# Low parts of the feed-forward weights by an accumulating DMA instead of a VectorE subtraction

## The chip, the cores and the metric

The kernel runs on one core of one Trainium2 chip. The metric is the device time of one execution in microseconds, the median of several runs. The core has five engines that run their own instruction streams and wait for each other by semaphores: PE (TensorE, matrix products; its weight loads are listed as PEld), DVE (VectorE), ACT (ScalarE), POOL (GpSimd) and SP (SyncE, which only issues DMAs here). Sixteen DMA engines move data between HBM and the on-chip memory SBUF. Products are summed in PSUM banks.

## The reference

Two transformer-like blocks on one sequence of 512 tokens with 1024 features, in float32. The first block has two layers: a convolution module in the first, attention with forget gates in the second, and after each of them the same feed forward and a gated projection:

```
hn = rmsnorm(h, ffn_norm[i])
h = h + jnp.square(jax.nn.relu(hn @ ffn_w1[i])) @ ffn_w2[i]      # 1024 -> 4096 -> 1024
```

The second block has three branches (a gated linear recurrence, block attention, attention to a memory), merges them and ends with a gated feed forward:

```
g = causal_dwconv(h @ w_ffn_gate, ffn_conv_w, ffn_conv_b)         # 1024 -> 3072
x = x + (jax.nn.gelu(g) * (h @ w_ffn_up)) @ w_ffn_down
```

The weights come in as float32.

## The kernel before, in words

**Products.** Activations lie feature-major: a tile is 128 features by 512 tokens. A float32 product is done with float32r operands, a shorter format: weight and activation are each split into a high part (rounded to float32r) and a low part (what rounding left), and `mm3` (line 356) issues three matmuls: high times high, high times low activation, low weight times high activation. `gemm` does this for the 8 k tiles of one output tile, so an output tile takes 24 matmuls.

**Panels.** All weights come in panels of 128 partitions by 2048 columns (1 MB), listed in the order of their use by `_panel_keys`. A panel of the feed forward holds 8 k tiles of 256 columns, so two output tiles, 48 matmuls. The feed-forward kinds are `w1` and `w2` (32 each over the two layers; for each of four chunks, four panels of `w1` and then four of `w2`), `gu` (24, a gate tile and an up tile each) and `dn` (12).

**How a panel gets ready.** `load` has SP fetch the raw panel into one of two raw buffers. `splitting` cuts it into four pieces of 512 columns; for each piece `part` has ScalarE copy the raw piece to `hi` (which rounds it) and VectorE, or for some kinds GpSimd, write `raw - hi` to `lo`. `hi` and `lo` have two buffers each. `panel(key)` makes sure that the split of this panel has been issued, and then calls `prefetch(i + 1, PREFETCH)`, which issues the load of the panel after the next and starts the split of the next one 3.0 us later.

**What sets the order.** Every engine executes its instructions in the order in which the program issues them. A planner, the class `Flow`, weaves them: it keeps an estimate of each engine's time, and side work (splits, norms, evacuations) is a generator that yields what its next step waits for. `flow.quiet(act, low, patience=HOLD)` lets a step go when the engines named are about free by the estimate, or after 1.2 us. These estimates only decide the order; what an instruction waits for on the chip are its real inputs.

**Around the panels.** `pairs` goes through the panels of a stage; in a stage's first panel the k tiles are the outer loop (`couter`), so that the panel can begin before all its input tiles are there. In the feed forward (line 826), VectorE takes the output tile out of PSUM (`z`), ScalarE squares it and rounds it, VectorE makes its low part. Norms run beside: ScalarE squares the stream's tiles (`sq`), GpSimd adds the squares up, VectorE makes the last addition, and PE forms the mean (`tp<-C,sq`). At the start of the second layer's feed forward the first `w1` panel's split is started by a `prefetch` with delay 0, behind the first half of the output projection's last tiles. The last two `dn` panels go token half by token half (256 columns): both panels for the first half, then both for the second; here `panel` of the last but one starts the split of the last.

Of the kernel before, what the change touches and what calls it, by code (L numbers as in the profile page):

```python
# [9 lines left out]
F32R = mybir.dt.float32r  # L10
BF = mybir.dt.bfloat16
AF = mybir.ActivationFunctionType
ALU = mybir.AluOpType
AX = mybir.AxisListType

S = 512
# [8 lines left out]

# [1 line left out]
_VECS = [  # L27
# [45 lines left out]
class Engine:  # L73
    """an engine whose instructions are issued in the order of the trace, with an estimate of when each one ends"""

# [48 lines left out]
class Flow:  # L124
    """Weaves side work into the stream of matrix products. Every engine issues in the order of this trace; a side is
    a generator that yields what its next step waits for: a time (us), tiles, or a condition."""

# [99 lines left out]
def kernel(ctx: ExitStack, tc, gain0, x_t, p_t, mem_t, vec, w, w_f, w_lru, rows, consts, out):  # L227
# [53 lines left out]

# [1 line left out]
    V = cp.tile([128, NV], F32, name="V")  # L283
# [11 lines left out]

# [1 line left out]
    raws, parts = {}, {}  # L297
# [9 lines left out]
    def part(i, k, pieces, low):  # L307
        """piece k of a panel's split, its low part on engine low"""
        if k == 0:
            parts[i] = tuple(wp.tile([128, PW], F32R, name=nm(n), tag=n, bufs=2) for n in ("hi", "lo"))  # L310
        r, (hi, lo), c = raws[i], parts[i], PW // pieces
        s = slice(c * k, c * k + c)
        gain = GAINED.get(_KEYS[i][0])
        if gain is not None:
            g = col(gain, k)
            act.activation(hi[:, s], r[:, s], AF.Copy, scale=g)
            dve.scalar_tensor_tensor(lo[:, s], r[:, s], g, hi[:, s].bitcast(F32), op0=ALU.mult, op1=ALU.subtract)
        else:
            act.copy(hi[:, s], r[:, s])
            low.tensor_sub(lo[:, s], r[:, s], hi[:, s].bitcast(F32))  # L320

    def splitting(i):
        pieces = KT if _KEYS[i][0] in GAINED else 4
        low = pool if _KEYS[i][0] in LO_POOL else dve
        c = PW // pieces
        for k in range(pieces):
            yield raws[i][:, c * k:c * k + c]
            yield flow.quiet(act, low, patience=HOLD)
            part(i, k, pieces, low)
# [17 lines left out]
    def panel(key, fetch=True):  # L347
        i = _PIDX[key]
        if i not in ahead:
            ahead[i] = flow.spawn(splitting(i), 0.0, 2)  # L350
        flow.finish(ahead[i])
        if fetch:
            prefetch(i + 1, PREFETCH)
        return parts[i]
# [6 lines left out]
    def gemm(ps, pan, c0, xs, width=256, ks=None, m=128):  # L361
        """ps += panel columns (from c0 of each k tile)^T x; ks: the k tiles of this call"""
        hi, lo = pan
        n = len(xs)
        for k in range(n) if ks is None else ks:
            if xs[k] is None:
                flow.until(lambda: xs[k] is not None)
            a = k * width + c0
            mm3(ps, hi[:, a:a + m], lo[:, a:a + m], xs[k][0], xs[k][1], k == 0, k == n - 1)

    def couter(pan, xs, ks=None, banks=None):
        """both output tiles of a panel, k tile by k tile"""
        banks = banks or [bank(), bank()]
        for k in range(len(xs)) if ks is None else ks:
            for j in range(2):
                gemm(banks[j], pan, 128 * j, xs, ks=[k])
        return banks

    def pairs(keys, xs):
        """output tiles of the panels in turn; the first panel k tile by k tile, while x still comes"""  # L380
        for i, key in enumerate(keys):
# [9 lines left out]

# [1 line left out]
    def split(src, g=None, n=S, scale=None):  # L393
        """exact two-part float32r split of src * g (g per feature)"""
        xh, xl = slot(F32R, "xh"), slot(F32R, "xl")
# [8 lines left out]
    def split_into(dst, k, src, g=None):  # L404
        """the same in steps, into dst[k]"""
        n = src.shape[-1]
# [12 lines left out]
    class Norm:  # L419
        """per-token mean over features of squares"""  # L420

# [48 lines left out]
    class Front:  # L470
        """input of a stage: gained splits of the stream's tiles as they come, and the norm's factor"""

# [36 lines left out]

# [1 line left out]
    G0 = cp.tile([128, KT], F32, name="G0")  # L511
# [32 lines left out]
    def diagonals(fs):  # L544
        """diagonal matrices of the last PE_TAPS[f] taps of a tile, both parts"""
        for f in fs:
# [27 lines left out]
    def conv_dve(order):  # L574
        """two tiles at a time, tap by tap in turn, so that none waits for its own sum; sums in PSUM"""
        todo, active = list(order), []
# [112 lines left out]

    # products that wait for nothing of the stream: ple projections, memory keys and values  # L690
    prd = dp.tile([KT, 128, S], F32, name="prd")

    def gemm32(ps, raw, c0, xs, width, m=128):
        """float32 products as they are, for panels whose splitting would hold other engines up"""
        n = len(xs)
        for k in range(n):
            a = k * width + c0
            pe.matmul(ps, raw[:, a:a + m], xs[k], start=k == 0, stop=k == n - 1)
# [61 lines left out]

    # layer norm over features, two passes
    ys = [None] * KT
# [56 lines left out]

# [1 line left out]
    def squared(z, k, t):  # L821
# [37 lines left out]

# [1 line left out]
    def diag(t, i):  # L861
        """query block i of transposed probabilities: key block j, query block i lies at column 384 j + 128 i"""
        a = t[:, 128 * i:128 * i + 128]
        return bass.AP(tensor=a.tensor, offset=a.offset, ap=[a.ap[0], [384, i + 1], [1, 128]])

    class Head:
        """causal attention of the head in rows 64 half.. of kt() and qt(); out() [128, S] takes a pair of heads"""

# [137 lines left out]
        def weigh(self):  # L1006
            """out[64 rows] = values^T probabilities^T; [V_hi | V_lo] or [V_lo | V_hi]"""
            vs = self.vs()
# [22 lines left out]
    class MemHead(Head):  # L1031
        """attention of one head of 128 features to the memory"""

# [48 lines left out]
    def attend(heads, period, gap):  # L1082
        """scores head by head, at least a period apart; all that follows as its inputs come"""
        state = {"scored": 0}
# [17 lines left out]
    def values(key, xs, r4):  # L1102
        """token-major values of 4 heads, split: per key block [128, 512]"""
        pan = panel(key)
        vs = []
        for b in range(4):
            ps = bank()
            token_major(ps, pan, xs, b)
            t = slot(F32R, "v")
            # heads 0,2: [hi|lo]; heads 1,3: [lo|hi]  # L1110
            v5 = t.rearrange("p (a b c d) -> p a b c d", a=2, b=2, c=2)
# [8 lines left out]

# [1 line left out]
    # the stream's tiles go in as they are, the gains into the weights; h is the sum of the two parts again  # L1122
    xs = front.xs
# [141 lines left out]

# [1 line left out]
    gg = small(8, "gg")  # L1267
# [47 lines left out]

    # gated linear recurrence
    xa, ga = [None] * 4, [None] * 4
# [10 lines left out]
    def recurrence():  # L1328
        # -8 softplus(-lam)
        lam = V[:, _VOFF["lam"]:_VOFF["lam"] + 4]  # L1330
# [53 lines left out]
        for f in range(4):  # L1384
# [4 lines left out]
            yield q  # L1389
            # 1 - a^2 = -tanh(log a) (1 + a^2)  # L1390
            dve.scalar_tensor_tensor(th[f], q, 1.0, th[f], op0=ALU.add, op1=ALU.mult)
# [24 lines left out]

    # block attention: of two blocks of 256 keys the past one is always chosen, so every earlier key counts
    rw, rr_ = slot(p="rows"), slot(F32R, "rowsr")
# [65 lines left out]

    # memory cross attention
    qx = [None] * 4
# [22 lines left out]

    # gated feed forward with a causal convolution on the gate  # L1510
    norms = [Norm(HALF) for _ in range(2)]
# [35 lines left out]

    # the last two panels token half by token half: the first one's norm and output go beside the second's products
    pre = [slot(p="out") for _ in range(2)]
# [64 lines left out]
MEM_PERIOD = 9.0  # L1614
LO_POOL = ("pw1", "vm", "o")


# [1 line left out]
def _pack(inp):  # L1619
# [3 lines left out]
    def wide(m, c0, n):  # L1623
        """columns c0..c0+n of m [K, N] as [128, K/128 * n]"""
        k = m.shape[0] // 128
# [96 lines left out]

    # shapes alone: identity, causal mask, 1/1024, distance rows
    consts = np.zeros((128, 257), np.float32)
# [41 lines left out]
```

## Time and profile before

| | |
|---|---|
| median of 3 runs | 2154.78 us (2154.36 to 2157.05) |
| profiled execution, span from first to last instruction | 2154.4 us |
| PE busy | 2109.2 us, 98% |
| VectorE busy | 1270.6 us, 59% |
| ScalarE busy | 937.4 us, 44% |
| GpSimd busy | 370.5 us, 17% |
| bytes moved by DMA | 204.79 MB, mean 95 GB/s |
| mean granted TensorE clock | 0.993 |

The profiled execution's own time is its span, 2154.4 us; the fastest run took 2154.36. Busy time is the time in which an engine executes; matmuls are pipelined, so one lasts longer in the list (390 ns) than the distance to the next, and the distance is what counts. In the rows a group is `out<-in` by the names in the program with the buffer numbers left out: `lo<-raw,hi` is the subtraction, `hi<-raw` the cast, `mm<-xh,lo` a matmul of a weight's low part. All instructions have line 83, since one helper issues them. In brackets stands the idle time of the engine before an instruction and what ended it. The stretch view gives, for each stretch, the busy time of each engine in it, the granted clock of TensorE as a share of 2.4 GHz, the DMA engines' mean share and their rate.

### The profile page before, as it was taken

To read this page: it belongs to the slowest core of one execution; us is meant where nothing else is said; L and a number is where in the kernel's file an instruction comes from. 1 tells how busy PE (TensorE), PEld (TensorE's weight loads), DVE (VectorE), ACT (ScalarE), POOL (GpSimd) and SP (SyncE) were. 2 spreads that over 40 slices of the span, in tenths; PEclk is the share of its full clock that TensorE was granted. 3 is DMA by queue.
4 is the path that set the end of the run, shared out by engine and by line. 5 is a ranking of instruction groups with operands and counts; after the bars stand their busy time and mean duration, and the time that the engine had idled before them with its cause. 6 is when DMAs were issued, how large, how long until landed. Compare 5 with 4: busy or idle time off the path is not lost. (4 is left out here: it accounts for less than half of the span.)

```text
span 2154.4 us, 26102 instructions
## 1 busy us (share of the span) xinstructions
PE 2109.2 (98%) x9920; PEld 1741.6 (81%) x9920; DVE 1270.6 (59%) x2166; ACT 937.4 (44%) x1884; POOL 370.5 (17%) x380
## 2 busy tenths in 40 slices
PE   7999999999999999999999999999999999999998
PEld 6867888888878887788888887778888888888887
DVE  5997534344576887544343567775564556465563
ACT  5766423233446676433232453665452333232222
POOL 5881100000121336300000031331010010000002
PEclk9999999999999999999999999999999999999999
DMA  5215232232222111222222233112222422222221
GB/s 183 98 45 190 86 110 80 97 104 92 98 80 85 61 61 60 79 98 98 98 93 89 95 125 129 71 64 95 98 79 79 142 93 98 100 96 98 95 101 59
DMA packets 38444, 204.79 MB, mean 95 GB/s; under 512 B 4648, under 2 KB 7976, under 8 KB 15920
## 3 DMA queue, kind: packets, MB, share of 16 engines
q1 hardware_dynamic: 37744, 202.62, 26.8%
q8 instruction: 78, 1.28, 0.2%
q10 hardware_dynamic: 576, 0.52, 0.1%
q14 instruction: 46, 0.38, 0.1%
HBM read 195.45 MB, written 7.68 MB: 94 GB/s over the span
## 5 line engine op out<-in xcount | busy, mean ns | idle before, releaser
L83 PE MATMUL mm<-xh,hi 128*128 128x512 f32 (+1 forms) x2544 | 991.5, 390 | 9.3 <-ACT hi L83 8.4
L83 PE MATMUL mm<-xl,hi 128*128 128x512 f32 (+1 forms) x2544 | 990.5, 389 | 0.0
L83 PE MATMUL mm<-xh,lo 128*128 128x512 f32 (+1 forms) x2544 | 990.0, 389 | 0.2
L83 PEld LDWEIGHTS mm<-xh,hi 128*128 128x128 f32 x2544 | 480.2, 189 | 105.0 <-ACT hi L83 8.4
L83 PEld LDWEIGHTS mm<-xh,lo 128*128 128x128 f32 x2544 | 480.1, 189 | 96.5 <-DVE lo L83 1.5
L83 PEld LDWEIGHTS mm<-xl,hi 128*128 128x128 f32 x2544 | 480.2, 189 | 94.3
L83 ACT CAST hi<-raw 128x512 fp32r<-128x512 f32 x636 | 354.3, 616 | 288.6 <-PE mm L83 268.9
L83 DVE TENSOR_TENSOR lo<-raw,hi 128x512 fp32r<-128x512 f32 x584 | 387.9, 713 | 50.3 <-ACT hi L83 48.8
L83 POOL TENSOR_TENSOR sq<-sq,sq 128x512 f32<-128x512 f32 (+1 forms) x69 | 84.7, 1230 | 1330.0 <-ACT sq L83 1329.4
L83 DVE TENSOR_TENSOR h<-mm,h 128x512 f32<-128x512 f32 (+1 forms) x113 | 75.6, 671 | 279.7 <-PE mm L83 279.6
L83 ACT ACTIVATE z<-z 128x512 f32<-128x512 f32 x64 | 40.4, 631 | 205.3 <-DVE z L83 205.3
L83 DVE SCALAR_TENSOR_TENSOR z<-mm,rbc 128x512 f32<-128x512 f32 x64 | 44.0, 690 | 120.7 <-PE mm L83 120.7
L83 POOL TENSOR_SCALAR P<-P,s 128x128 f32<-128x128 f32 (+2 forms) x112 | 65.3, 588 | 243.6 <-DVE s L83 151.0
L83 DVE TENSOR_TENSOR t<-mm,rbc 128x512 f32<-128x512 f32 x80 | 54.9, 688 | 82.5 <-PE mm L83 78.7
L83 DVE TENSOR_TENSOR xl<-z,xh 128x512 fp32r<-128x512 f32 x64 | 44.3, 693 | 74.7 <-ACT xh L83 74.7
L83 ACT ACTIVATE t<-t 128x512 f32<-128x512 f32 x40 | 25.2, 631 | 128.5 <-DVE t L83 128.4
L83 POOL TENSOR_TENSOR acc<-acc,tap 128x482 f32<-128x482 f32 (+29 forms) x60 | 77.3, 1288 | 13.1 <-ACT tap L83 9.5
L83 DVE SCALAR_TENSOR_TENSOR sc<-u,V,sc 128x511 f32<-128x511 f32 (+21 forms) x116 | 78.9, 732 | 0.5
L83 ACT ACTIVATE xh<-h,V 128x512 fp32r<-128x512 f32 x40 | 28.6, 722 | 112.4 <-DVE h L83 112.4
L83 POOL TENSOR_TENSOR lo<-raw,hi 128x512 fp32r<-128x512 f32 x52 | 69.6, 1363 | 38.8 <-ACT hi L83 38.6
L83 ACT CAST pth<-ptp 128x128 fp32r<-128x128 f32 (+2 forms) x112 | 46.1, 418 | 53.2 <-PE ptp L83 52.6
L83 ACT ACTIVATE P<-sc,s 128x128 f32<-128x128 f32 (+2 forms) x112 | 58.5, 524 | 18.1 <-DVE s L83 17.4
(228 smaller groups left out, 2235.8 us busy)
## 6 DMA issues: line engine op xcount, KB each, us to landing
raw<-in_w SPq DMA_DIRECT2D x175, 1024.0 KB
h<-in_x_t SPq DMA_DIRECT2D x8, 256.0 KB
prd<-pr SPq DMA_DIRECT2D x8, 256.0 KB
pr<-prd SPq DMA_DIRECT2D x8, 256.0 KB
resid<-h SPq DMA_DIRECT2D x8, 256.0 KB
h<-resid SPq DMA_DIRECT2D x8, 256.0 KB
out<-out SPq DMA_DIRECT2D x12, 128.0 KB
raw<-in_w SPq DMA_DIRECT2D x4, 256.0 KB
```

Source lines behind the costliest of these rows:

```text
L83: f(out, *args, **kw)
```

## The change

For the kinds `w1`, `w2`, `gu` and `dn`, the split goes another way. ScalarE writes `-raw` to the float32r tile `lo`, which rounds it, so that the tile holds minus the high part; after each two of the four pieces GpSimd issues a DMA that adds the raw weights, read from HBM a second time, to these 1024 columns. Then ScalarE makes the four casts to `hi`. VectorE has no part in it. `lo` gets three buffers for all kinds. A split of these kinds starts 0.2 us after its `prefetch`, not 3.0 us. The planner gets an estimate for the accumulating DMA. Comments and docstrings are taken out as well (not shown).

```diff
     def part(i, k, pieces, low):
         if k == 0:
-            parts[i] = tuple(wp.tile([128, PW], F32R, name=nm(n), tag=n, bufs=2) for n in ("hi", "lo"))
+            parts[i] = tuple(
+                wp.tile([128, PW], F32R, name=nm(n), tag=n, bufs=b) for n, b in (("hi", 2), ("lo", 3)))
...
+    def accumulate(out, src):
+        nc.gpsimd.dma_start(out, src, accum_op=ALU.add)
+        n = 4 * (out.size() if callable(out.size) else out.size)
+        flow.dma_t = max(flow.dma_t, flow.now, flow.when([out])) + n / 175e3
+        for k in flow.spans(out):
+            flow.ready[k] = flow.dma_t + 2.5
+
+    def splitting_dma(i):
+        r = raws[i]
+        parts[i] = hi, lo = tuple(
+            wp.tile([128, PW], F32R, name=nm(n), tag=n, bufs=b) for n, b in (("hi", 2), ("lo", 3)))
+        c = PW // 4
+        cut = [slice(c * k, c * k + c) for k in range(4)]
+        for k in range(4):
+            yield r[:, cut[k]]
+            yield flow.quiet(act, patience=HOLD)
+            act.mul(lo[:, cut[k]], r[:, cut[k]], -1.0)
+            if k % 2:
+                two = slice(c * k - c, c * k + c)
+                yield lo[:, two]
+                accumulate(lo[:, two], w[i, :, two])
+        for k in range(4):
+            yield flow.quiet(act, patience=HOLD)
+            act.copy(hi[:, cut[k]], r[:, cut[k]])
+
     def splitting(i):
+        if _KEYS[i][0] in LO_DMA:
+            yield from splitting_dma(i)
+            return
...
         if fetch:
-            prefetch(i + 1, PREFETCH)
+            prefetch(i + 1, 0.2 if _KEYS[min(i + 1, len(_KEYS) - 1)][0] in LO_DMA else PREFETCH)
...
+LO_DMA = ("w1", "w2", "gu", "dn")
```

## Rows read from the trace of the kernel before

**Rows 1.** Page, part 1: engine, busy us, share of the span, instructions.
```profile
PE 2109.2 (98%) x9920; PEld 1741.6 (81%) x9920; DVE 1270.6 (59%) x2166; ACT 937.4 (44%) x1884; POOL 370.5 (17%) x380
```

**Rows 2.** Stretches: length, busy PE PEld DVE ACT POOL (count), clock, DMA share, GB/s.
```profile
300.00:360.00 60.00, 60.00 (x266) 49.73 (x265) 23.16 (x37) 16.90 (x30) 0.00 (x0) 1.00 0.28 99
```

**Rows 3.** The same view, one panel of the first feed forward.
```profile
348.00:358.88 10.88, 10.88 (x49) 9.01 (x49) 5.18 (x8) 4.59 (x8) 0.00 (x0) 1.00 0.26 98
```

**Rows 4.** Page, part 5: costliest groups, busy us, mean ns, idle before, releaser.
```profile
L83 PEld LDWEIGHTS mm<-xh,lo 128*128 128x128 f32 x2544 | 480.1, 189 | 96.5 <-DVE lo L83 1.5
L83 ACT CAST hi<-raw 128x512 fp32r<-128x512 f32 x636 | 354.3, 616 | 288.6 <-PE mm L83 268.9
L83 DVE TENSOR_TENSOR lo<-raw,hi 128x512 fp32r<-128x512 f32 x584 | 387.9, 713 | 50.3 <-ACT hi L83 48.8
L83 ACT ACTIVATE xh<-h,V 128x512 fp32r<-128x512 f32 x40 | 28.6, 722 | 112.4 <-DVE h L83 112.4
```

**Rows 5.** Stretch view, entry of the second layer's feed forward.
```profile
906.04:913.90 7.86, 7.86 (x27) 6.89 (x28) 1.91 (x4) 0.24 (x2) 1.39 (x1) 0.50 0.41 146
```

**Rows 6.** Timeline there: start us, us, engine, operation, count [idle before <-releaser].
```profile
889.15 0.61 ACT L83 CAST hi<-raw 128x512 fp32r<-128x512 f32 x1
...
892.36 1.28 DVE L83 TENSOR_TENSOR lo<-raw,hi 128x512 fp32r<-128x512 f32 x2
897.56 1.18 DVE L83 TENSOR_TENSOR lo<-raw,hi 128x512 fp32r<-128x512 f32 x1
900.36 1.77 DVE L83 TENSOR_TENSOR lo<-raw,hi 128x512 fp32r<-128x512 f32 x1
...
893.20 8.39 POOL L83 TENSOR_TENSOR sq<-sq,sq 128x512 f32<-128x512 f32 x5 [2.57 <-ACT sq L83]
908.18 1.39 POOL L83 TENSOR_TENSOR s<-s,mhalf 128x4 f32<-128x4 f32 x1 [6.60 <-DVE s L83]
...
894.17 0.39 PE L83 MATMUL mm<-xh,hi 128*128 128x512 f32 x1
894.62 0.39 PE L83 MATMUL mm<-xh,lo 128*128 128x512 f32 x1
906.04 1.86 PE L83 MATMUL tp<-C,sq 128*128 128x1 f32 x8 [4.68 <-DVE sq L83]
...
902.16 0.33 SPq L279 DMA_DIRECT2D raw<-in_w  x1
```

**Rows 7.** Timeline of the last two panels.
```profile
2119.53 0.28 PE L83 MATMUL mm<-xh,hi 128*128 128x256 f32 x1
2125.28 0.28 PE L83 MATMUL mm<-xh,hi 128*128 128x256 f32 x1
...
2121.09 0.60 ACT L83 CAST hi<-raw 128x512 fp32r<-128x512 f32 x1
...
2122.95 0.68 DVE L83 TENSOR_TENSOR lo<-raw,hi 128x512 fp32r<-128x512 f32 x1
...
2121.02 1.44 POOL L83 TENSOR_TENSOR sq<-sq,sq 128x256 f32<-128x256 f32 x2 [4.00 <-ACT sq L83]
```

**Rows 8.** Timeline of a panel of the first feed forward.
```profile
348.69 0.69 DVE L83 SCALAR_TENSOR_TENSOR z<-mm,rbc 128x512 f32<-128x512 f32 x1 [2.59 <-PE mm L83]
...
350.61 2.18 ACT L83 CAST hi<-raw 128x512 fp32r<-128x512 f32 x4
...
353.87 0.33 SPq L279 DMA_DIRECT2D raw<-in_w  x1
```

**Rows 9.** Stretch view, first and last half us of a load's bytes.
```profile
903.00:903.50 0.50, 0.00 (x0) 0.00 (x0) 0.39 (x1) 0.50 (x2) 0.00 (x0) 1.00 0.71 131
...
906.00:906.50 0.50, 0.46 (x3) 0.46 (x3) 0.50 (x1) 0.08 (x1) 0.00 (x0) 0.50 0.44 180
```

**Rows 10.** Timeline of PE, end of the first layer.
```profile
641.81 1.02 PE L83 MATMUL tp<-C,sq 128*128 128x1 f32 x8 [1.77 <-DVE sq L83]
```

## The prediction

> **What bounds the kernel now.** I read the page's first part, then stretches of 60 us, then the places where PE is not full. The first part has PE busy 98% of the span and DVE 59% [rows 1]: the engine that the change relieves isn't the fullest. In the stretches where the changed panels run, PE is busy for all 60.00 of 60 us and starts 266 matmuls [rows 2], one per 0.226 us; a panel of 48 lasts 10.88 us, and in one such panel PE is busy throughout, with VectorE at 5.2 us and ScalarE at 4.6 [rows 3]. Over the whole run PE's weight loads of `lo` stood idle 96.5 us, but VectorE's `lo` ended only 1.5 us of that [rows 4]. So in the middle of a feed-forward stage a quicker low part buys nothing, and the question is where it comes late. Two places differ from the middle: the entry of the second layer's feed forward, after which the clock is granted at 0.50, the 1.2 GHz level [rows 5], since PE stands 4.68 us for a VectorE sum [rows 6], and the last two panels, used up in half the time [rows 7].
>
> **The change part by part.** 100 panels are concerned (32 w1, 32 w2, 24 gu, 12 dn).
>
> *Removed:* four VectorE subtractions a panel, 400 of the 584 of mean 713 ns [rows 4], 285 us of VectorE. In the steady panels they lie beside a full PE: worth 0. What they pay at the entry comes below.
>
> *Added on ScalarE:* four multiplications by -1 a panel. The trace has none of that form; I price them as the cast of the same tile, 616 ns alone [rows 4], 2.18 us for four in a row [rows 8]. Ends: 2.18 and 2.9 us (four at the 722 ns of a scaled activation [rows 4]). ScalarE's 4.6 us a panel becomes 6.8 to 7.5 of 10.88. The casts to `hi` now stand behind the multiplications. With the split starting 0.2 us after a panel begins (348.7 by the evacuation in rows 8), not 3 us after, they end by about 356, and PE wants them at 359.6: covered with 3.6 us to spare. The raw load two panels on waits for these casts and no longer for VectorE, so it goes out at about 356 where it went at 353.87 [rows 8]; it needs 4.3 us (below), perhaps 7 beside other traffic, and is wanted at 370.6. Covered.
>
> *Added on GpSimd's queue:* two accumulating DMAs a panel, half a MB each, 200 in all; no row has one. A plain 1 MB load is issued at 902.16 [rows 6], its bytes begin by about 903.0 and end by about 906.4 [rows 9]: 0.85 us and 3.5 us. One panel's load takes 0.26 of 10.88 us [rows 3], 2.83 us of all engines. Lower end: an accumulating MB costs what a plain one does, 3.5 us. Upper end: it reads HBM, reads the tile and writes it one after another, three passes, 10.5 us. I take two passes, 7 us a panel, because a sum has two operands where the plain load has one, and both write one. For the issue on GpSimd I take the 0.33 us of SP's, at most the 1.39 us of GpSimd's smallest instruction, a power of four columns [rows 6].
> The Trainium skill, "Collectives: The Full Stack", section on the bandwidth ceiling, puts the ratio at 1.93 since an adding transfer reads two sources. By that a panel's accumulation would be 6.8 us, and the sum would stay as it is; no row of this trace shows it.
>
> In the steady panel: two multiplications end by 350.6, the first half's bytes run 351.5 to 355.0, the second half's to 358.5; with the slow issue, 359.6. PE reads the first low part 0.45 us into the next panel (360.0), the second half 12 matmuls later (362.7). Slack 5 and 4 us, 3 at the slow issue. ScalarE doesn't wait for a buffer there, as `lo` has three. Cost: 0. With three passes the halves land at 356.8 and 362.0, still in time, but load and accumulation together ask 4 x 2.83 = 11.3 us of engines in a 10.88 us panel. That is the upper end: 0.44 us a panel over 98 panels, +43 us; if traffic never packs better than in a single load (4 x 3.5 = 14.0), +305.
>
> *Entry of the second layer's feed forward.* The first w1 panel's split starts behind the last output tiles. Its first cast stood at 889.15, and PE read `hi` at 894.17 and `lo` at 894.62 [rows 6]. Now the multiplications take the casts' slots, at most 1.2 us apart by the patience in the code, and the casts come behind them, the first at about 895. The first DMA goes out at about 891.3 (GpSimd's sums begin at 893.20 [rows 6]) and lands 4.35 us later, 895.7, or 896.8 at the slow issue. A **new wait** of 1 to 3 us, take 2.6. The second half is issued between GpSimd's five sums (8.39 us from 893.20), which hold it back until 896 to 898: landing 900.4 to 903.4; PE wants it 24 matmuls after its start, 902.2. What is queued behind the waiting DMA on GpSimd is these sums of squares, and PE waits for their last. What goes: VectorE's low parts from 892.36 on (1.28 + 1.18 + 1.77 = 4.2 us [rows 6]) stood in the chain that PE waited for until 906.04. That chain moves up to 902 or 903, held by GpSimd's sums (to 901.6); PE, begun 2.6 us late, is at that point at about 904: the 4.68 us are gone. What is late next is the landing of the second half. Net 2.6 - 4.7 = -2.1 us, if the new wait lowers the clock as the old one did. PE was at 0.50 for 7.86 us [rows 5], in which half, 3.9 us, was lost. If the clock holds: -6.0. If the low part lands 4 us later: +2.
>
> *End.* The last panel but one begins at 2119.53 and runs with 256 columns, so it's over at 2125.28, after 5.75 us and not 10.88 [rows 7]. Before, the last panel's split was just in time: its first cast at 2121.09, its first `lo` at 2122.95. Now: multiplications from 2119.7, with squares between; the second ends at 2121.0. GpSimd has two sums from 2121.02 to 2122.5, before or behind the DMA. The first half lands between 2125.4 and 2128.2; PE wants it two matmuls in, at 2125.52. The second lands 3.5 us behind it, 2128.9 to 2131.7, and is wanted at 2125.52 + 12 x 0.12 = 2127.0. Waits of 1.9 to 4.7 us in sum, directly on the path that ends the kernel; take +3.3. If an accumulating DMA is as quick as a plain one, the second half lands at 2127: 0. If the clock falls in that wait as at the entry: 4.7 + 4.0 = +8.7.
> GpSimd's sums stretched VectorE's `lo` at 900.36 to 1.77 us [rows 6] against the mean of 713 ns, so these two engines do get in each other's way. The Trainium skill, "SBUF — State Buffer", in the section "A bandwidth-pool intuition that's wrong", has a VectorE copy keep GpSimd from writing the descriptors of its DMA, so that 620 ns become 3100. By that the end would cost up to 2.5 us more, 2158.5 in all; no row of this trace shows a GpSimd DMA.
>
> **Sum** against the profiled execution's own time, for which I take its span, 2154.4 us: steady 0, entry -2.1, end +3.3, so 2155.6. The median of the runs is 2154.78, 0.4 above; forecast **2156 us**, no change. A measurement of this kernel can tell 0.2%, 4.3 us, from nothing.
>
> **Rivals.**
> *A, the accumulation doesn't keep pace* (slower; it decides from 10.88 - 2.83 = 8.05 us a MB). For it: twice as many bytes, half of them added to a second operand, and no such row. Against: the DMA engines are idle 74% of a panel. At three passes 2154.8 + 43 = 2198; the far end 2460. Chance 0.23.
> *B, the edges are late* (slower): entry +2, end +8.7, so 2165. For it: the panel at the end is half as long and the lead isn't; a wait that lowers the clock costs twice. Against: the waits come in pieces, and one of 1.77 us in the first layer [rows 10] was followed by a full clock. Chance 0.17.
> *C, VectorE's relief shows* (faster): the entry keeps its clock, -6.0, and the end is quick, 0: 2149. For it: 4.2 us of low parts in the chain that PE waits for. Against: GpSimd's sums hold that chain too, and the new wait stands ahead of it. Chance 0.17.
> *The forecast*: the edges cancel, 2151 to 2160. Chance 0.43. VectorE's load falls as the change says, and nobody waited for it.
>
> **How the numbers follow.** Faster by 0.2%: C, and a little of the forecast's lower edge, 0.18. Same: 0.40 of the forecast's 0.43. Slower: A, B and the forecast's upper edge, 0.42. The range leaves out nearly 2 in 10: 0.07 below 2148 (an entry with more than C's gain), 0.11 above 2215 (A with more than three passes' cost).
>
> **What would show it.** VectorE's busy time down by about 285 us, ScalarE's up by 220 to 290. Right: PE still at 60.00 of 60 us between the entries; a PE wait for a DMA of about 2.6 us at the first w1 panel of the second layer, and none of 4.7 us behind it; one or two of together 3.3 us at the last panel. Wrong: PE waits for `lo` in panel after panel (A), a DMA share of over 0.7 in the stages, casts that PE waits for (ScalarE late), or no waits at the edges and a time below 2150.

## The result, and the profile after

The changed kernel takes 2168.98 us (median of 4 runs, 2166.20 to 2170.15) against 2155.32 us for the kernel before: ratio 1.0062, 95% interval [1.0051, 1.0074], 13.7 us **slower**. A second set of five runs gave 2168.82 against 2155.55, ratio 1.0061 [1.0048, 1.0074]. The time lies in the range that was forecast, but not in the likeliest case, no change (2151 to 2160). The profiled execution took 2166.20 us and its span is 2164.4: a run is 1.8 us longer than its span.

The work moved as the change says. Part 1 of the page after, answering to [rows 1]:

```profile
PE 2110.5 (98%) x9920; PEld 1740.7 (80%) x9920; DVE 1023.2 (47%) x1766; ACT 1143.5 (53%) x2284; POOL 540.6 (25%) x580
```

VectorE gave up 247 us and ScalarE took on 206. PE's busy time hardly differs, since it does the same matmuls. The same stretches as in [rows 2, 3], then three of the entry and four of the last stage (length, busy PE PEld DVE ACT POOL with counts, granted clock, DMA share, GB/s):

```profile
300.00:360.00 60.00, 60.00 (x266) 49.68 (x265) 11.05 (x16) 27.36 (x50) 8.73 (x11) 1.00 0.78 186
348.00:358.88 10.88, 10.88 (x50) 9.01 (x49) 2.77 (x4) 6.69 (x13) 1.73 (x3) 1.00 0.79 194
...
890.00:900.00 10.00, 4.74 (x18) 3.07 (x16) 8.56 (x10) 9.71 (x19) 7.41 (x6) 0.89 0.33 52
900.00:910.00 10.00, 9.51 (x34) 7.98 (x35) 0.85 (x2) 2.42 (x6) 4.65 (x5) 0.60 0.87 199
...
1754.00:1780.00 26.00, 23.32 (x107) 19.04 (x107) 9.60 (x15) 12.48 (x22) 4.57 (x5) 1.00 0.45 111
1780.00:1805.00 25.00, 25.00 (x112) 20.67 (x111) 10.88 (x17) 10.62 (x20) 3.49 (x4) 1.00 0.96 226
...
1900.00:1930.00 30.00, 28.76 (x124) 22.84 (x123) 13.06 (x19) 15.91 (x32) 5.42 (x6) 1.00 0.88 211
...
2030.00:2060.00 30.00, 29.04 (x127) 23.39 (x126) 14.88 (x23) 15.94 (x30) 5.46 (x6) 1.00 0.82 191
```

Two things are to be seen. In the first feed forward PE is as full as before although the DMA engines' share rose from 0.26 to 0.79: a steady `w1` or `w2` panel costs nothing. In the last stage (`gu`, `dn`) PE loses 2.68, 1.24 and 0.96 us at the full clock, each near the beginning of one of the three chunks. The kernel before loses nothing there:

```profile
1754.00:2120.00 366.00, 366.00 (x1621) 303.33 (x1620) 209.53 (x321) 105.34 (x191) 2.87 (x4) 1.00 0.27 95
```

PE's waits in the kernel after (us in total, times, longest):

```profile
PE tp L83 <- DVE sq L83: 12.0, 8, 4.3
PE mm L83 <- ACT hi L83: 11.9, 2, 7.7
PE mm L83 <- DMA lo<-in_w: 6.4, 6, 2.7
```

The third line is new. In the second, 7.72 us are the program's start and 4.15 us are new. The accumulating DMA's price, by the page's parts 3 (packets, MB, share of 16 engines), 5 (as in [rows 4]) and 6 (KB each, median us to landing):

```profile
q0 software_dynamic: 28800, 104.87, 28.0%
q1 hardware_dynamic: 37744, 202.62, 26.0%
...
L83 PEld LDWEIGHTS mm<-xh,lo 128*128 128x128 f32 x2544 | 480.3, 189 | 106.0 <-DMA lo<-in_w 9.7
L83 ACT ACTIVATE lo<-raw 128x512 fp32r<-128x512 f32 x400 | 219.6, 618 | 0.0
...
lo<-in_w POOLq DMA_DIRECT2D x200, 512.0 KB, 7.9
```

q0 is GpSimd's queue. An accumulating MB holds the engines for 28.0/104.87 against 26.0/202.62 of a plain one: 2.1 times, the two passes of the prediction. (Against plain DMAs in GpSimd's own queue, which took 15.9% in the run e_plain below, it is 1.8 times.) But half a panel lands 7.9 us after its issue, not the 4.35 worked out there. The multiplication costs 618 ns.

**A steady panel**, as in [rows 8] (timeline: start us, us, engine, operation, count, and in brackets the idle time before and what ended it):

```profile
346.25 2.19 ACT L83 ACTIVATE lo<-raw 128x512 fp32r<-128x512 f32 x4
349.55 2.18 ACT L83 CAST hi<-raw 128x512 fp32r<-128x512 f32 x4 [1.11 <-PE mm L83]
...
347.69 0.86 POOL L325 DMA_DIRECT2D lo<-in_w  x1 [14.41 <-ACT lo L83]
348.73 0.86 POOL L325 DMA_DIRECT2D lo<-in_w  x1 [0.18 <-issue]
```

The panel before ends at about 349.5, when its `hi` buffer comes free and the casts go. The multiplications need no buffer of PE's, and ran 3.3 us ahead of that: this lead pays for the longer landing.

**The entry of the second layer**, as in [rows 6]:

```profile
888.40 0.62 ACT L83 ACTIVATE lo<-raw 128x512 fp32r<-128x512 f32 x1
890.14 0.62 ACT L83 ACTIVATE lo<-raw 128x512 fp32r<-128x512 f32 x1
893.24 0.61 ACT L83 ACTIVATE lo<-raw 128x512 fp32r<-128x512 f32 x1
894.38 0.61 ACT L83 ACTIVATE lo<-raw 128x512 fp32r<-128x512 f32 x1
897.07 2.16 ACT L83 CAST hi<-raw 128x512 fp32r<-128x512 f32 x4
...
892.44 1.71 POOL L83 TENSOR_TENSOR sq<-sq,sq 128x512 f32<-128x512 f32 x1 [2.57 <-ACT sq L83]
894.09 0.91 POOL L325 DMA_DIRECT2D lo<-in_w  x1
894.75 4.94 POOL L83 TENSOR_TENSOR sq<-sq,sq 128x512 f32<-128x512 f32 x3
899.63 0.88 POOL L325 DMA_DIRECT2D lo<-in_w  x1
...
897.72 0.73 PE L83 MATMUL mm<-xh,hi 128*128 128x512 f32 x1 [4.15 <-ACT hi L83]
900.49 0.80 PE L83 MATMUL mm<-xh,lo 128*128 128x512 f32 x1 [1.61 <-DMA lo<-in_w]
```

The multiplications take the slots of the casts, which stood from 889.15 on, and the casts come at 897.07. PE waits 4.15 us for them and 1.61 for the DMA, which went out only at 894.09, behind the sum of squares from 892.44. The wait of 4.68 us is gone, but the new ones lower the clock just as it did (0.89 and 0.60 in the stretches above).

**The beginning of a `gu` chunk:**

```profile
1764.82 0.63 ACT L83 ACTIVATE t<-t 128x512 f32<-128x512 f32 x1 [6.10 <-DVE t L83]
1765.36 1.14 ACT L83 ACTIVATE lo<-raw 128x512 fp32r<-128x512 f32 x2
...
1770.87 0.63 ACT L83 ACTIVATE t<-t 128x512 f32<-128x512 f32 x1 [3.87 <-DVE t L83]
1771.41 1.14 ACT L83 ACTIVATE lo<-raw 128x512 fp32r<-128x512 f32 x2
...
1766.79 0.92 POOL L325 DMA_DIRECT2D lo<-in_w  x1 [11.30 <-ACT lo L83]
1772.85 0.87 POOL L325 DMA_DIRECT2D lo<-in_w  x1 [5.14 <-ACT lo L83]
...
1779.27 0.50 PE L83 MATMUL mm<-xh,lo 128*128 128x512 f32 x1 [2.68 <-DMA lo<-in_w]
```

Here ScalarE is free and yet late: it executes in order, and the multiplications stand behind a Gelu (`t<-t`) that waits up to 6.10 us for VectorE's convolution. The second half's DMA goes out at 1772.85, and PE stands for it until 1779.27. The chain of waits passes here in each of the three chunks; in the third:

```profile
2036.39 0.76 DVE t L83
2037.72 2.17 ACT hi L83 x4
2039.88 1.06 ACT lo L83 x2
2041.23 0.88 POOL lo L325
2042.79 12.17 DMA lo<-in_w
2055.00 86.61 PE mm L83 x433
```

Where DMAs bunch, one takes 12.17 us.

**The end**, as in [rows 7]; the last panel but one begins at 2128.14:

```profile
2125.48 2.18 ACT L83 ACTIVATE lo<-raw 128x512 fp32r<-128x512 f32 x4
...
2126.92 0.89 POOL L325 DMA_DIRECT2D lo<-in_w  x1 [1.29 <-ACT lo L83]
2127.96 0.88 POOL L325 DMA_DIRECT2D lo<-in_w  x1 [0.16 <-issue]
...
2157.49 1.96 ACTq L1600 DMA_DIRECT2D out<-out  x4
```

The same last row of the kernel before:

```profile
2149.40 1.96 ACTq L1569 DMA_DIRECT2D out<-out  x4
```

No matmul waits for a low part at the end. But from the start of this last group of four output issues to the end of the span it is 6.9 us, 5.0 in the kernel before; the DMA engines are idle in the last 3 us.

A ledger of where PE stands against the kernel before (profile against profile, us, + is later; by the matmuls that form a norm's mean and by one just before the entry, at their times in the kernel before, and by the span):

| at | after | again | e_lead | e_lead2 | b_entry | c_nolow |
|---|---|---|---|---|---|---|
| 101.90, past the start | +0.7 | 0.0 | +0.2 | -0.4 | +1.8 | +0.7 |
| 641.81, first feed forward done | +0.8 | +0.2 | +0.3 | -0.2 | +1.7 | +0.3 |
| 891.23, before the second entry | -0.8 | +1.4 | -1.3 | -0.3 | +3.0 | -1.3 |
| 1256.25, second one done | +0.9 | +3.1 | -3.5 | -5.2 | -2.7 | -8.2 |
| 1318.38, norms behind it | +0.9 | +3.1 | -3.1 | -5.0 | -2.5 | -5.9 |
| 1750.90, last stage's norm | +2.2 | +4.1 | -1.0 | -2.5 | -2.6 | -5.6 |
| 2132.84, last mean but one | +8.6 | +11.2 | -0.1 | -1.8 | -2.6 | -5.9 |
| span | +10.0 | +12.6 | +1.4 | +0.1 | -2.5 | -5.9 |

In the two profiles of the changed kernel, the last stage costs 6.4 and 7.1 us, the second feed forward with its entry 1.6 and 1.7 (from 891.23 to 1256.25), the stages between 1318.38 and 1750.90 1.3 and 1.0 (0.58 is a wait for VectorE's sums where the last stage begins), the end of the program 1.4 on balance. About 1.7 of the 7.1 us are a lower clock: a_again was granted 0.89 from 1774 to 1790, behind the first of the DMA waits, where the first profile has 1.00.

Two cautions. A run is 1.8 us longer than its span, so the profile of the kernel before stands for a run of about 2156.2 us, not 2154.4, 0.9 above the median of 2155.3; the ledger shows that much too little. And the clock falls in one profile and not in the next where the code is the same. The wait of 1.77 us at 641.81 [rows 10] was followed by a granted 1.00 from 642 to 652 in the kernel before, in the kernel after and in c_nolow, and by 0.83 in a_again, e_lead2 and b_entry; from 836 to 846 it is 0.83 in the kernel before, in a_again and in b_entry, and 1.00 in the other four. Each is worth about 1.7 us, and the columns change between 641.81 and 891.23 by little else. Over the entry itself e_gudn and e_one, which have the code of the kernel before there, differ from it by 0.6 and 0.7 us.

### The profile page after: what moved, and what is told of

The parts are those of the page before. It is cut to its first block, busy times and chain, and to the rows that moved or that the text cites. A ratio compares the mean times of both kernels' runs of the same rounds, so it can differ in the third digit from the quotient of the medians.

```text
span 2164.4 us, 26672 instructions
## 1 busy us (share of the span) xinstructions
PE 2110.5 (98%) x9920; PEld 1740.7 (80%) x9920; DVE 1023.2 (47%) x1766; ACT 1143.5 (53%) x2284; POOL 540.6 (25%) x580
## 3 DMA queue, kind: packets, MB, share of 16 engines
q0 software_dynamic: 28800, 104.87, 28.0%
q1 hardware_dynamic: 37744, 202.62, 26.0%
## 5 line engine op out<-in xcount | busy, mean ns | idle before, releaser
L325 POOL DMA_DIRECT2D lo<-in_w x200 | 174.4, 879 | 820.4 <-ACT lo L83 782.0
L83 ACT ACTIVATE lo<-raw 128x512 fp32r<-128x512 f32 x400 | 219.6, 618 | 0.0
L83 DVE TENSOR_TENSOR lo<-raw,hi 128x512 fp32r<-128x512 f32 x184 | 130.4, 737 | 31.7 <-ACT hi L83 29.8
```

The lines of the kernel that those rows point to most:

```text
L83: f(out, *args, **kw)
L325: nc.gpsimd.dma_start(out, src, accum_op=ALU.add)
```

## Experiments

Theory L: the low part is issued **too late** where ScalarE's order puts its multiplications behind work that waits. Theory T: the **traffic** that doubled costs by itself. Smaller theories: the relief of VectorE is worth something that is lost elsewhere; the queue has a fixed cost.

**c_nolow**, the kernel before without the subtraction for the four kinds: what VectorE's relief can bring at most.

```diff
...
             act.copy(hi[:, s], r[:, s])
-            low.tensor_sub(lo[:, s], r[:, s], hi[:, s].bitcast(F32))
+            if _KEYS[i][0] not in NO_LOW:      # w1, w2, gu, dn: lo is hi
+                low.tensor_sub(lo[:, s], r[:, s], hi[:, s].bitcast(F32))
```

> The kernel before, with the VectorE subtraction for w1, w2, gu and dn left out altogether (the matmuls of the low weights read the high part instead, so the output is not the reference's). It is the ceiling of any relief of VectorE here: 400 subtractions gone and nothing put in their place. Theory (nobody waits for these subtractions in the stages, only the entry of the second layer's feed forward can gain): 2147 to 2155 us, VectorE busy about 985 us, and no gain outside the entry. Rival (the relief was worth a good deal and the DMAs ate it): below 2140 us.

2151.41 against 2154.54 us, 0.9987 [0.9978, 0.9995]. Its stretch view at the entry:

```profile
880.00:960.00 80.00, 78.52 (x355) 64.96 (x354) 27.24 (x37) 34.47 (x61) 10.19 (x7) 1.00 0.27 94
```

The same of the kernel before:

```profile
880.00:960.00 80.00, 75.32 (x325) 62.38 (x324) 43.71 (x61) 33.45 (x59) 10.77 (x7) 0.94 0.25 88
```

PE waits 1.49 us there in place of 4.68 and keeps its clock: 6.9 us from 891.23 to 1256.25 by the ledger, of which 2.3 are lost again by 1318.38. (The 8.5 us that later expectations name count from 641.81 on, with 1.6 us of clock in front of the entry.) So about 3 us by the medians, inside the range that was expected, is all that taking the low parts off VectorE can be worth, and it is worth it at one place.

**e_one**, the kernel before with one accumulating DMA of 256 KB near the start, which nobody reads.

```diff
+    one = cp.tile([128, S], F32, name="one_acc")
+    pool.memset(one, 0.0)
+    nc.gpsimd.dma_start(one, w[9, :, :S], accum_op=ALU.add)
```

> The kernel before plus one single accumulating DMA from GpSimd, 256 KB, near the start, into a tile that nobody reads. Theory (using GpSimd's DMA queue at all costs a fixed amount at the end of the program: after's run is 1.8 us longer than its span where before's is equal to it, and its span has 1.4 us more after the last matmul): +3 us, 2158 us. Rival (what is lost goes with the number of DMAs): within 0.5 us of before, 2155 us.

2156.61 against 2154.54, 1.0010 [1.0001, 1.0019]; the span ends 5.06 us after the last group of output issues begins, as before. So a GpSimd queue has no fixed cost at the end of the program. The 2.1 us of the medians lie between theory and rival; 1.1 of them stand at 101.90 in its profile, within what profiles differ by there, and the rest isn't placed.

**e_w** and **e_gudn**, the change for two kinds each.

```diff
-LO_DMA = ("w1", "w2", "gu", "dn")
+LO_DMA = ("w1", "w2")                # e_w;  ("gu", "dn") in e_gudn
```

> The changed kernel with the accumulating DMAs for w1 and w2 only (64 of the 100 panels, 128 DMAs); gu and dn on VectorE again. Theory (fixed cost 3 us, the entries of the two layers +1, the rest of w1 and w2 free): 2158 to 2160 us, no PE wait for a DMA but at the entry of the second layer. Rival (the loss goes with the traffic): 64% of 13.7 us, 2164 us.

> The changed kernel with the accumulating DMAs for gu and dn only (36 panels, 72 DMAs). Theory (fixed 3 us, and about 7 to 8 us at the beginnings of the three gu chunks, where the multiplications stand behind the Gelu on ScalarE): 2165 to 2167 us. Rival (the loss goes with the traffic): 36% of 13.7 us, 2160 us.

e_w: 2158.44 against 2154.54, 1.0020 [1.0011, 1.0029], with one DMA wait (2.0 us) and the `hi` wait at the entry. e_gudn: 2161.46, 1.0035 [1.0022, 1.0048], with three DMA waits (4.5 us) and 7.1 us lost between 1750.90 and 2132.84. 64 panels of `w1` and `w2` cost 4 us, 36 of `gu` and `dn` cost 7: no price per panel. e_w came at the time that its theory gave, though the fixed 3 us in it aren't there; its entry costs 1.9 us from 891.23 to 1256.25, and the rest isn't placed. e_gudn lost in `gu` what was expected, but the fixed 3 us weren't there, so it stayed below the 2165 to 2167.

**e_lead**, the changed kernel with multiplications and DMAs issued a panel earlier than the casts; traffic is the same.

```diff
...
             ahead[i] = flow.spawn(splitting(i), delay, 2)
+            n = i + 1
+            if all(j < len(_KEYS) and _KEYS[j][0] in LO_DMA for j in (i, n)) and n not in lows:
+                lows[n] = flow.spawn(low_dma(n), delay, 2)   # multiplications and DMAs of n; casts stay
```

> The changed kernel with the multiplications and their accumulating DMAs of a panel issued one panel earlier (lo has three buffers, so this needs no more memory); the casts to hi stay where they are. The same instructions and the same bytes. Theory (at the beginnings of the gu chunks the multiplications stand behind the Gelu on ScalarE, so the DMA is issued too late): the PE waits for lo in the gu stage, 4.8 us in after's profile, go, and the time falls by 5 to 7 us against a_again, to about 2160. Rival (the accumulating DMAs are too slow or too many there, whenever they are issued): the waits stay, 2165 us or more.

**e_plain**, the changed kernel with plain DMAs in place of accumulating ones, so that `lo` holds the raw weights.

```diff
-        nc.gpsimd.dma_start(out, src, accum_op=ALU.add)
+        nc.gpsimd.dma_start(out, src)
```

> The changed kernel with plain DMAs in place of the accumulating ones (the raw weights overwrite lo, so the output is not the reference's): the same number, issue and order, but the tile isn't read back. Price of the accumulation: GpSimd's queue takes 28.0% of the engines' time in after; by the plain loads' 26.0% for 202.62 MB it would be 13.5%. Theory (the issue is late): the landing falls by 2 us or so, the worst gu wait of 2.68 us to 0.5 to 1 us, time 3 to 4 us below a_again. Rival (the accumulation's second read is what costs): all the gu waits go, 6 to 7 us below a_again.

**a_again**, the changed kernel as it is, in the same set.

> The changed kernel again, beside the others on one chip. 2164 to 2169 us (before 2154.5). Theory: 6 to 7 us of the difference lie between the first gu panel and the last dn panel, as in its first profile (+6.4), the entry of the second layer's feed forward is worth nothing in sum, about 1 us each at the start and at the first entry.

In this set the kernel before takes 2155.55 us, a_again 2168.82, e_lead 2159.30 (1.0019 [1.0010, 1.0028]) and e_plain 2162.76 (1.0032 [1.0019, 1.0045]). PE's waits in e_lead:

```profile
PE mm L83 <- ACT hi L83: 10.2, 2, 8.1
PE mm L83 <- DMA lo<-in_w: 3.2, 2, 2.3
```

Its only DMA waits are 2.30 us at the entry and 0.86 on the last panel. The last stage costs 0.9 us, not 7.1, with the same bytes in the same queue (28.1% of the engines, landing after 8.1 us). So T falls as the cause: 9.5 of the 13.3 us are the late issue. Part of them is won at the entry, where e_lead gains 2.1 us and a_again loses 1.7. In e_plain the queue takes this share, and a transfer this time to land:

```profile
q0 software_dynamic: 28800, 104.87, 15.9%
...
lo<-in_w POOLq DMA_DIRECT2D x200, 512.0 KB, 5.4
```

At the same late issue the last stage then costs 0.3 us, and one wait of 0.37 us is left in `gu`. This is what the rival of that expectation said, not its theory. The second pass is thus what makes lateness hurt: both are needed, and either taken away frees the stage. Of the 7.2 us that e_plain is still slower than the kernel before, 4.1 come behind the last output (see the last section).

**i_lag**, the kernel before with each norm's mean 4 us later in the issue order, for the rival that the gain at the entry needs no DMA.

```diff
         def chain(self):
             yield self.norm.sum
+            yield FRONT_LAG
...
+FRONT_LAG = 4.0
```

> The kernel before with one line more: the mean of a stage's norm is issued on PE 4.0 us later by the planner's clock, so that PE does more products before it waits for VectorE's sum. Nothing of the change is in it. Theory (what c_nolow won, 8.5 us by PE's position at the entry, was the wait of 4.68 us and the half clock behind it, not VectorE's time as such): the waits of 4.68 and 3.95 us shrink to 1 us or less, the clock stays at 1.00 there, 2140 to 2148 us. Rival (the factor comes later for the evacuations, and PE waits for banks instead): 2154 us or more.

2158.29 against 2155.55, 1.0012 [1.0003, 1.0021], not the 2140 to 2148 that were expected. The 4.68 us at the entry go (waits of 0.73, 0.34 and 1.36 come there), but in the stretch 1280 to 1340 PE is busy for 53.46 us where it was 56.05, at a clock of 0.89 where it was 0.94. A lag everywhere moves the wait rather than removing it.

**b_entry** and **e_lead2**, to use what was found. e_lead2 leads for the first panel of each stage too; b_entry does so for four `w1` panels at the second layer's entry, and leaves all others as before but for the third `lo` buffer. Against e_lead:

```diff
-            if all(j < len(_KEYS) and _KEYS[j][0] in LO_DMA for j in (i, n)) and n not in lows:
+            if n < len(_KEYS) and _KEYS[n][0] in LO_DMA and n not in lows:     # e_lead2
+            if n < len(_KEYS) and by_dma(n) and n not in lows:                 # b_entry
                 lows[n] = flow.spawn(low_dma(n), delay, 2)
...
-LO_DMA = ("w1", "w2", "gu", "dn")                                              # b_entry: by_dma in its place
+def by_dma(i):
+    return i < len(_KEYS) and _KEYS[i][:3] == ("w1", 1, 0)
```

> The kernel before, with the accumulating DMA for the four w1 panels of the second layer's first chunk alone, and the multiplications of each, the first too, issued one panel ahead of its casts; the casts stand where they stood. Theory: what the change costs is the late issue of the multiplications on ScalarE, and what VectorE's subtractions cost before is the second layer's entry (4.68 us of waiting and half the clock for about 8 us). Then PE waits there for neither hi nor lo, the stretch 880 to 960 us is granted 1.00, PE is 8.5 us earlier behind it, of which the attention stage takes back 2.5, as in the kernel without low parts: about 2149.5 us, ratio 0.997 to 0.998, faster than both kernels. Rival: the accumulating DMA itself is in the way there, by its GpSimd instruction in front of the sums of squares or by its bytes beside the loads; then PE still waits 2 us or more for the sums or the low part, the clock falls to 0.50 again, and the time is 2153 to 2157.

> The changed kernel with the multiplications and accumulating DMAs one panel ahead of the casts everywhere, at the first panel of each stage too (the version measured earlier led only inside the stages, and took 2159.3). Theory of the late issue: the waits that were left there, 2.09 us for hi and 2.30 us for lo at the second layer's entry and 0.6 us at the first layer's, go; the entry comes to -8.5 us as in the kernel without low parts, of which 2.5 come back in the attention stage: 2159.3 - 4.8 + 2.5 - 0.6 = about 2156, ratio 1.000 to 1.001. Rival: doubled traffic costs by itself wherever it flows; then the first panels wait although they lead, and the time stays at 2158 to 2161.

The kernel before takes 2155.26 here. b_entry takes 2151.85, ratio 0.9988 [0.9979, 0.9996]: faster than the changed kernel, and than the kernel before by 0.1%, near the limit of what these runs can tell. Its entry:

```profile
880.00:960.00 80.00, 77.58 (x349) 63.89 (x348) 34.36 (x50) 41.20 (x75) 17.73 (x16) 1.00 0.55 145
```

PE waits 1.04 us for the sums there, the clock holds, and 5.7 us are won between 891.23 and 1256.25, of which 5.5 are left at 1318.38. The forecast of 8.5 was too high: c_nolow itself won only 6.9 there, and here PE waits 1.38 us for the low part of the second panel, at 915.91. e_lead2 takes 2154.87, ratio 0.9996 [0.9987, 1.0004]: no change, 14 us better than the changed kernel. It still waits 2.08 us for the second `w1` panel's low part at 913.39, whose DMA stood behind GpSimd's sums of squares until 901.10.

## Why the prediction was partly right

**Luck.** The range held 2169 only because it was drawn up to 2215 for rival A, engines that don't keep pace. That is not what happened, and what cost the most, the late issue in `gu`, is in none of the rivals.

**Right.** PE bounds, and steady panels cost nothing where the split's lead is as in [rows 8]: from 918 to 1250 PE's distance to the kernel before stays at 0.86 us. The multiplication (618 ns for 616, 2.19 us for 2.18) and the two passes (2.1 times a plain MB, 1.8 against plain DMAs of the same queue) were priced about right. The Trainium skill, "Collectives: The Full Stack", section on the bandwidth ceiling, has 1.93 between an AllGather and a ReduceScatter, which reads two sources to add; the 2.1 and 1.8 of these runs lie on either side of it. GpSimd's DMA instruction took 0.87 us (174.4 us for 200), between the 0.33 and 1.39 set as ends. The Trainium skill's "SBUF — State Buffer", section "A bandwidth-pool intuition that's wrong", has a DMA of GpSimd's take 3100 ns in place of 620 beside a VectorE copy. Here the issue at 894.09 took 0.91 us and the longest of the 200 took 1.25; VectorE ran sums and products beside them and no copies, so the page's own case is not tested. VectorE's relief was 247 us, not 285: in the list its subtractions overlap, so that 584 of mean 713 ns are 387.9 us of busy time [rows 4] and not 416. The sign "a DMA share of over 0.7" came (0.78) and cost nothing there: the prediction's own two passes give 3 x 2.83 of 10.88 us, which is 0.78, so the sign was set too low.

**Wrong: "Slack 5 and 4 us ... Cost: 0", taken for all 98 panels.** That slack was read from one `w1` panel. In `gu` the multiplications stand behind a Gelu that waits for VectorE, and the slack is gone: 6.4 us (7.1 in the second profile, with the lower clock), of which 4.8 are DMA waits in the trace; the rest shows as no wait. Half of the same step, the landing of 4.35 us, was mis-sized too: it took a single load's duration in quiet, and beside the panel's own load it is 7.9, up to 12.8 where they bunch. In `w1` and `w2` that was covered by something else that the prediction missed, multiplications that run 3.3 us before the panel begins.

**Wrong: the entry.** Forecast -2.1 with a wait of 2.6 us for the DMA; measured +1.6 and +1.7, with 4.15 for `hi` and 1.6 to 1.8 for the DMA. The first DMA, put at about 891.3, went out at 894.09 behind one of GpSimd's sums. The displacement of the casts was seen (about 895; it was 897.07) and not priced as a wait of its own. That the new wait would lower the clock was right.

**Wrong: the end.** Forecast +3.3, measured no wait for a low part, for the reason just named: the last split ran 2.7 us before the panel in front of it began, and not after. In its place came 1.9 us behind the last output, which no row of before could show.

**The sum's base** lacked the 1.8 us between a span and a run; this moves 2155.6 to 2157.4 and decides nothing. Rival A was wrong, since the DMA engines keep pace at a share of 0.79. B's size, 2165, was nearest, and its entry (+2) came with 1.6 and 1.7; its end (+8.7) did not, and the rest lay in the `gu` chunks. What was said against B, that a wait of 1.77 us was followed by a full clock, was chance: in a_again the same wait was followed by 0.83. C's gain at the entry is real, as b_entry shows, once the low part leads.

## What to carry to other kernels

A slack read in one steady panel holds for that panel's neighbours on the engine, not for another stage: look at what stands in front of the moved instruction on its in-order engine in every stage that it enters. Work that needs only a raw input and its own buffer can be issued a whole panel early, and that, with the same bytes, is what hid a transfer of 8 to 13 us here. Relief of an engine that isn't the bound is worth what it brings at the few places where PE waits for that engine; moving four panels there did at least as much as moving a hundred.

## What was not expected of the hardware

From the start of the last group of output issues to the end of the span it takes 5.0 to 5.1 us in the kernels with 0, 1, 8, 72 and 128 DMAs on GpSimd's queue, 6.9 in the four with 200 accumulating ones, and 9.1 with 200 plain ones. The DMA engines are idle in the added time; what ends it stays open. The start differs from profile to profile too: the first 40 us were granted 0.96 in the kernel before and 0.91 in the kernel after, in i_lag and in b_entry, and PE stands up to 1.8 us later behind them in the ledger. In a_again, the changed kernel once more, they were granted 0.96 and PE stands at 0.0, so this is no part of the change. Nor is it the clock alone: c_nolow was granted 0.96 and stands at +0.7.

An equal wait doesn't always have an equal sequel. Behind the 1.77 us at 641.81 the clock held in some executions and fell in others, to a mean of 0.83 over the stretch from 642 to 652; behind the same 4.68 us at the entry the stretch from 880 to 925 was granted 0.89 in the kernel before and 0.92 in e_gudn and e_one. So a gain in clock read from one pair of profiles is known to 1 or 2 us only.
